# Scores of the first attention layer as three products in half-height tiles, with splits over all partitions and a new order of the program

## The chip, the cores and the metric

The kernel runs on one core of a Trainium2 chip. The metric is device time in microseconds (us) of one execution. The engines are TensorE (PE for its matrix products, PEld for its loads of the stationary operand), VectorE (DVE), ScalarE (ACT), GpSimd (POOL) and SyncE (SP), whose queue issues nearly all DMAs.

## The reference, cut to what matters

Two layers over 256 tokens of width 1024, 16 heads of 64. The change touches the scores of layer 0 (block attention; with 256 tokens there is one block, so it is plain causal attention):

```python
q = rope(rms_norm(split_heads(q, N_HEADS), q_gain), pos)     # per head 256 x 64
k = rope(rms_norm(split_heads(k, N_HEADS), k_gain), pos)
s_own = jnp.einsum('bhcd,bhkd->bhck', qc, k_own)             # scores, contraction of 64
m_own = jnp.broadcast_to(k_pos[None, :] <= q_pos[:, None], (B, H, C, MOBA_BLOCK))
pr = masked_softmax(s * scale, m)
o = merge_heads(pr @ v) * jax.nn.silu(z)
x = x + o @ w_out
gate = jax.nn.sigmoid(rms_norm(x, ple_gate_gain[i]) @ ple_w_gate[i])
x = x + gate * (p[i] @ ple_w_proj[i])
```

Layer 1 is the NSA mixer (compressed, selected and window branches) with the same output and gate parts. Gains of the norms are about 8, so scores are large and are computed to nearly full float32 accuracy.

## The kernel before, in words

Products run in the type fp32r. To keep accuracy every float32 operand is split in two: hi, the value rounded to fp32r (one ScalarE copy), and lo, the rest (one VectorE subtraction); a product is then hi x hi + lo x hi + hi x lo. Weights arrive in pieces of 128 x 1024 (`raw`), are split into `hi` and `lo` tiles of five buffers each, and are multiplied with the split activations `a`, into four PSUM banks named `mm`. PSUM banks `s` (two) take scores, banks `tr` (two) transposes and the products with the values.

Nothing is issued in the order in which it is written. The kernel records all its operations in a `Plan`. `PROGRAM` (line 26) names some 500 steps; where a step stands there sets the priority of its operations. `schedule` (line 263) goes through the operations with costs for each (`cost`, line 187) and places on every engine the one that can start first. A switch of PE between tile shapes is charged there (line 347), and `together` (line 243) keeps a list of operations next to each other on PE. So an edit of a cost or of `PROGRAM` can move any instruction of the kernel; line 399 issues them all, which is why every row of the profile has that line.

Layer 0's attention goes by eight `Pair`s of heads (line 982), each in three steps, and four value steps `V0` to `V3`:

- `A` transposes q and k of two heads into one `tr` bank: head 0 on partitions 0 to 63, head 1 on 64 to 127, columns q (256) then k (256). `stack_moba` (line 968) then builds, for each head j, a tile `qk[:, j]` with the head's hi on its own half of the partitions and its lo on the other half, and a tile `k2` with the halves of k exchanged. That takes two ScalarE copies of 64 x 512, two VectorE subtractions of 64 x 512 and four copies of 64 x 256, which the planner gives to ScalarE or VectorE.
- `S` (line 997) computes, for each head j and each half t of the tokens, two products over all 128 partitions: `qk` x `qk` (hi hi + lo lo) and `qk` x `k2` (the two mixed terms). For t = 0 they have 128 columns, for t = 1 256. That is eight products a pair, `together` by twos. The softmax's maximum and exponential follow on VectorE and ScalarE (`block_exp`, tile `sm`).
- `T` (line 1019) transposes the exponentials into `pt`.
- `V` (`pairs_pv`, line 852) multiplies with the values in tiles of 64 columns, two heads alternating between halves of the array's columns. Plain float32 products such as these show as two records each.

The scores of layer 1 (line 1174) use stacked tiles in the same way as `stack_moba` and are not edited.

Of the kernel before, what the change touches and what calls it, by code (L numbers as in the profile page):

```python
# [7 lines left out]
F32 = mybir.dt.float32  # L8
# [5 lines left out]
P = 128  # L14
T = 256
# [4 lines left out]
SWITCH, POW = 150.0, 2300.0  # L20
NRAW, NHI, NLO, NPT, NA = 5, 5, 5, 9, 9
WARM = 16
WIDE, NARROW = "o0 o1 g0 g1 no0 no1 ng0 ng1", "ng1b"
MARGIN = 100.0

PROGRAM = ("x0 w:c0 c0 x1 w:c1 c1 x2 w:c2 x3 w:c3 x4 w:c4 w:k.0 x5 c2 w:c5 c3 x7 consts tq a.1 x6 a.3 a.5 a.6 w:c6 a.7 w:c7 "
# [24 lines left out]

STORES = 5

# [55 lines left out]
class Plan:  # L109
# [77 lines left out]
    def cost(self, op, views, first):  # L187
        n = first.elems() if isinstance(first, View) else 0
        e, m = op.engine, op.method
        if m == "dma_start":  # L190
            v = first if isinstance(first, View) else op.args[1]
            return v.elems() * 4 * v.ap.ap[0][1]
        if e == "tensor":
            k, c = op.args[1].ap.ap[0][1], op.args[1].ap.ap[1][1]
            op.mode = tuple(128 if x > 64 else 64 if x > 32 else 32 for x in (k, c))
            if m == "transpose":
                return 109.2
            if op.args[1].ap.dtype == mybir.dt.bfloat16:
                return n / 2.4
            if op.args[1].ap.dtype == F32R:  # L200
                return (n + 32) / 2.4 if n > 128 else 110

            return 2 * max(54.6 if op.mode == (128, 64) else 109.2, 2 * n / 2.4 / (2 if op.mode == (128, 64) else 1))
        if e == "gpsimd":
            if op.kwargs.get("op") == OP.pow:
                return (POW if n < 16 else 1300.0) + 130.0 * n
            return 100 + 2.3 * n
        psum = any(self.tags[v.tile.tag]["psum"] for v in views)
        rows = first.ap.ap[0][1]
        half = 110 if rows in (60, 64) and (any(v.box()[0] != first.box()[0] for v in views)  # L210
                                            or psum and first.ap.dtype == F32R and m == "activation") else 0
        if e == "scalar":
            if first.tile.tag == "early":
                return 1500.0
            c = (60 if psum else 110) + 0.833 * max(n, op.args[1].elems())
            return half + c + 93 * sum(isinstance(op.kwargs.get(k), View) for k in ("scale", "bias", "accum_out"))
        if m == "tensor_tensor_reduce":
            return 130 + 1.04 * n
        if m == "reciprocal":
            return 65 + 6.9 * n  # L220
        if m == "tensor_reduce":
            return 65 + 1.04 * op.args[1].elems()
        two = len([v for v in views if v.elems() > 2 and v is not first]) > 1
        if not psum and not two and m in ("tensor_copy", "tensor_scalar"):
            return 70 + half + 0.52 * n + 60 * any(isinstance(x, View) and x.elems() == 1 for x in op.args[2:])
        if m == "tensor_tensor" and args_step(op.args[1]) >= 16:
            return 65 + 1.75 * n
        return 65 + half + 1.055 * n + (65 if m == "scalar_tensor_tensor" and isinstance(op.args[2], View) else 0)
# [192 lines left out]
def trunk(ctx: ExitStack, tc: tile.TileContext, a, out):  # L421
# [543 lines left out]
    def masks_():  # L965
        nc.hold_on(lambda: load_consts(384, CST_N), at["w:" + BEHIND.split()[1]])

    def stack_moba(ps):

        qk = work.tile([P, 1024], F32R, tag="hl", name="qk").rearrange("p (j c) -> p j c", j=2)  # L970
        k2 = work.tile([P, 512], F32R, tag="qk", name="k2").rearrange("p (j c) -> p j c", j=2)
        own = [slice(0, HD), slice(HD, P)]
        for j in range(2):
            o = own[j]
            nc.scalar.activation(qk[o, j], ps[o], AF.Copy)
            nc.vector.tensor_tensor(qk[own[1 - j], j], ps[o], qk[o, j].bitcast(F32), op=OP.subtract)
        for j in range(2):
            nc.copy(k2[own[1 - j], j], qk[own[j], j, T:])
            nc.copy(k2[own[j], j], qk[own[1 - j], j, T:])
        return qk, k2  # L980

    class Pair:


# [4 lines left out]
        def A(self):  # L989
            ps = bank("tr", 2)  # L990
            for i, s in enumerate((self.half.Q, self.half.K)):
                for t in range(2):
                    nc.tensor.transpose(ps[:, (2 * i + t) * P:(2 * i + t + 1) * P],
                                        s[:, t, 2 * self.p:2 * self.p + 2].rearrange("p a d -> p (a d)"), ident)
            self.qk, self.k2 = stack_moba(ps)

        def S(self):
            qk, k2 = self.qk, self.k2
            self.l = work.tile([P, 2, 2], F32, tag="l", name="l")
            ss, self.sm = [bank("s", 2) for _ in range(2)], []  # L1000
            for j in range(2):
                for t in range(2):
                    since = len(nc.ops)
                    for x in range(2):
                        n = t * P + P
                        nc.tensor.matmul(ss[j][:, cuts[t]], qk[:, j, t * P:n], k2[:, j, 0:n] if x else qk[:, j, T:T + n],
                                         start=x == 0, stop=x == 1)
                    nc.together(since)
            for j in range(2):
                sm = work.tile([P, 384], F32, tag="sm", name="sm", bufs=5)  # L1010
                self.sm.append(sm)
# [515 lines left out]
```

## Time and profile before

| | us |
|---|---|
| median of three runs (359.20, 359.52, 360.35) | 359.52 |
| profiled execution, its own time | 360.45 |
| profiled execution, its span | 358.7 |

The span runs from the first to the last instruction of the profiled execution. PE, PEld, DVE and ACT below are busy times; matrix products are pipelined, so a record's duration (some 0.28 us for 256 columns) is longer than the distance to the next start (0.12 us), and it is the distance between starts that tells what a product costs. In groups, `out<-in` names tiles, `128*64` the rows and columns of the array that a product uses, `128x256` the shape of its result; the last two columns are busy us with the mean ns of one, and the idle time before it. `s<-hl` and `s<-qk,hl` are the score products, `tr<-pt,v` the value products, `mm` the projections. In layer 0, `hl` is the buffer of `qk`, and `qk` that of `k2`.

### The profile page before, as it was taken

How to read it: one execution, taken by the hardware profiler on the slowest of the kernel's cores; microseconds unless marked ns; L12 is line 12 of the kernel's file. 1: busy time of each engine (PE TensorE's matmuls, PEld its weight loads, DVE VectorE, ACT ScalarE, POOL GpSimd, SP SyncE). 2: the span in 40 equal slices, each digit the busy share in tenths (PEclk: the TensorE clock that was granted, in tenths of full speed). 3: DMA queues.
4: the chain of work that ended last, by engine and by line, in shares of the span. 5: the costliest groups of instructions: out<-in, count | busy, mean ns of one | idle time of the engine just before them, and what ended most of it. 6: DMA issues, size and time to landing. Idle time of an engine off the chain costs nothing.

```text
span 358.7 us, 6738 instructions
## 1 busy us (share of the span) xinstructions
PE 351.5 (98%) x2329; PEld 308.9 (86%) x2329; DVE 333.9 (93%) x845; ACT 276.2 (77%) x614; POOL 29.1 (8%) x26
## 2 busy tenths in 40 slices
PE   6999999999999999999999999999999999999995
PEld 5888888888999888888889999866998989888885
DVE  3999989999999988989999999999999999999985
ACT  3976599998999864758853988978989999956632
POOL 1033300321000000000004300003000000000100
PEclk9999999999999999999999999999999999999999
DMA  7999665053653456664443725347674332167012
GB/s 219 320 366 275 217 211 192 32 158 133 212 178 116 132 172 172 184 215 147 166 131 95 258 66 174 119 137 273 238 222 156 118 106 74 58 191 221 0 47 73
DMA packets 20770, 58.95 MB, mean 164 GB/s; under 512 B 2560, under 2 KB 6016, under 8 KB 20736
## 3 DMA queue, kind: packets, MB, share of 16 engines
q1 hardware_dynamic: 20160, 58.04, 50.0%
q10 hardware_dynamic: 576, 0.48, 0.4%
q8 instruction: 18, 0.29, 0.3%
q14 instruction: 16, 0.13, 0.1%
HBM read 57.46 MB, written 1.05 MB: 163 GB/s over the span
## 4 chain that ended last, share of the span: by engine, by line
PE 96%; DMA 2%; DVE 0%; ACTq 0%; issue 0%; ACT 0%; DVEq 0%
PE mm L399 77%; PE tr L399 13%; PE s L399 6%; DMA tmp<-in_moba_in 2%; ACTq L399 0%; DVE tmp L399 0%; DVE hi L399 0%; ACT tmp L399 0%; DVEq L1522 0%; DVE xT L399 0%
## 5 line engine op out<-in xcount | busy, mean ns | idle before, releaser
L399 PE MATMUL mm<-a,hi 128*128 128x256 f32 (+1 forms) x656 | 163.4, 327 | 0.0
L399 ACT ACTIVATE hi<-raw 128x1024 fp32r<-128x1024 f32 (+2 forms) x100 | 99.7, 1008 | 35.2 <-PE mm L399 29.5
L399 PE MATMUL mm<-a,lo 128*128 128x256 f32 x448 | 125.5, 284 | 0.0
L399 DVE TENSOR_TENSOR lo<-raw,hi 128x1024 fp32r<-128x1024 f32 (+2 forms) x100 | 115.0, 1159 | 5.9 <-ACT hi L399 5.3
L399 PEld LDWEIGHTS mm<-a,hi 128*128 128x128 f32 x656 | 109.9, 190 | 10.6
L399 PE MATMUL mm<-hi,a 128*128 128x512 f32 (+2 forms) x356 | 101.7, 375 | 1.7 <-DVE hi L399 1.7
L399 PEld LDWEIGHTS mm<-a,lo 128*128 128x128 f32 x448 | 84.4, 190 | 0.6 <-DVE big L399 0.2
L399 PEld LDWEIGHTS mm<-hi,a 128*128 128x128 f32 x356 | 64.2, 190 | 12.8 <-ACT a L399 1.9
L399 PE MATMUL mm<-lo,a 128*128 128x512 f32 (+2 forms) x178 | 63.8, 374 | 0.0
L399 ACT ACTIVATE sm<-sm,nb 128x128 f32<-128x128 f32 (+1 forms) x96 | 42.6, 448 | 3.8 <-DVE nb L399 3.6
L399 PEld LDWEIGHTS mm<-lo,a 128*128 128x128 f32 x178 | 33.0, 188 | 5.4 <-DVE lo L399 0.2
L399 DVE CUSTOM_DVE_ANT_0 sm<-s,cst,nr_q 128x128 f32<-128x128 f32 (+1 forms) x96 | 35.7, 408 | 0.5 <-PE s L399 0.2
L399 ACT ACTIVATE pt<-tr 128x384 f32<-128x384 f32 x48 | 21.7, 484 | 0.6 <-PE tr L399 0.4
L399 ACT ACTIVATE tmp<-tmp 128x256 f32<-128x256 f32 (+3 forms) x26 | 12.1, 471 | 12.9 <-DVE tmp L399 12.7
L399 PE MATMUL tr<-cst,sm 128*128 128x128 f32 x144 | 22.0, 275 | 0.0
L399 POOL TENSOR_TENSOR r_q<-r,neg_half 128x16 f32<-128x16 f32 x5 | 14.6, 2922 | 77.3 <-DVE r L399 77.3
L399 PEld LDWEIGHTS tr<-cst,sm 128*128 128x128 f32 x144 | 16.9, 141 | 3.1 <-ACT sm L399 0.8
L399 ACT ACTIVATE a<-xT,gain_in 128x256 fp32r<-128x256 f32 x31 | 14.5, 498 | 5.2 <-DMA xT<-in_x 3.2
L399 DVE TENSOR_TENSOR hl<-tr,hl 64x512 fp32r<-64x512 f32 x24 | 16.5, 688 | 2.1 <-ACT hl L399 1.5
L399 ACT ACTIVATION_READ_ACCUMULATOR sm<-sm,nb 128x1 f32 x96 | 18.3, 191 | 0.0
L399 DVE TENSOR_SCALAR sm<-sm,l 128x128 f32<-128x128 f32 (+1 forms) x67 | 17.7, 314 | 0.1
L399 POOL TENSOR_TENSOR rstd<-ms,neg_half 128x2 f32<-128x2 f32 x4 | 3.9, 973 | 167.9 <-DVE ms L399 167.9
(167 smaller groups left out, 452.4 us busy)
## 6 DMA issues: line engine op xcount, KB each, us to landing
raw<-in_moba_in SPq DMA_DIRECT2D x28, 512.0 KB, 4.3
raw<-in_nsa_in SPq DMA_DIRECT2D x24, 512.0 KB, 4.5
raw<-in_w_o SPq DMA_DIRECT2D x8, 512.0 KB, 3.7
raw<-in_w_g SPq DMA_DIRECT2D x8, 512.0 KB, 3.9
raw<-in_w SPq DMA_DIRECT2D x8, 512.0 KB, 3.6
raw<-in_w_no SPq DMA_DIRECT2D x8, 512.0 KB, 4.0
raw<-in_w_ng SPq DMA_DIRECT2D x8, 512.0 KB, 4.2
raw<-in_ple_proj SPq DMA_DIRECT2D x4, 512.0 KB, 3.9
```

The source lines that it names most:

```text
L399: getattr(getattr(self.nc, o.engine), o.method)(*[real(x) for x in o.args], **{k: real(x) for k, x in o.kwargs.items()})
```

## The change

`stack_moba` goes. `A` now makes one tile `hl` of 128 x 1024: hi of the whole transposed bank (q and k of both heads, all partitions), then lo. `S` computes three products a head and token half, hi hi, lo hi and hi lo, each over the 64 partitions of its head, with the two heads in turn, and all twelve are kept together. The product lo lo is no longer computed.

```diff
-    def stack_moba(ps):
-        qk = work.tile([P, 1024], F32R, tag="hl", name="qk").rearrange("p (j c) -> p j c", j=2)
-        k2 = work.tile([P, 512], F32R, tag="qk", name="k2").rearrange("p (j c) -> p j c", j=2)
-        own = [slice(0, HD), slice(HD, P)]
-        for j in range(2):
-            o = own[j]
-            nc.scalar.activation(qk[o, j], ps[o], AF.Copy)
-            nc.vector.tensor_tensor(qk[own[1 - j], j], ps[o], qk[o, j].bitcast(F32), op=OP.subtract)
-        for j in range(2):
-            nc.copy(k2[own[1 - j], j], qk[own[j], j, T:])
-            nc.copy(k2[own[j], j], qk[own[1 - j], j, T:])
-        return qk, k2
...
-            self.qk, self.k2 = stack_moba(ps)
+            self.hl = work.tile([P, 1024], F32R, tag="hl", name="hl").rearrange("p (x c) -> p x c", x=2)
+            nc.scalar.activation(self.hl[:, 0], ps, AF.Copy)
+            nc.vector.tensor_tensor(self.hl[:, 1], ps, self.hl[:, 0].bitcast(F32), op=OP.subtract)
...
-            for j in range(2):
-                for t in range(2):
-                    since = len(nc.ops)
-                    for x in range(2):
-                        n = t * P + P
-                        nc.tensor.matmul(ss[j][:, cuts[t]], qk[:, j, t * P:n], k2[:, j, 0:n] if x else qk[:, j, T:T + n],
-                                         start=x == 0, stop=x == 1)
-                    nc.together(since)
+            since = len(nc.ops)
+            for t in range(2):
+                n = t * P + P
+                for q, k in ((0, 0), (1, 0), (0, 1)):
+                    for j in range(2):
+                        r = slice(j * HD, j * HD + HD)
+                        nc.tensor.matmul(ss[j][:, cuts[t]], self.hl[r, q, t * P:n], self.hl[r, k, T:T + n],
+                                         start=q == k, stop=k == 1)
+            nc.together(since)
```

The planner's cost of an fp32r product is halved when the tile has 64 rows and 128 columns, and `PROGRAM` is another list from the step `masks` on; before it, both lists are the same. One line of each, from the start of layer 0's attention:

```diff
-           "w:1q.0 w:1q.3 1q.0 masks w:1k.0 A2 S2 w:1k.2 w:1q.1 w:1q.2 A3 1k.0 1k.1 w:1v.0 S3 1q.1 1q.2 1q.3 1qe A0 1q T2 "
+           "w:1q.0 w:1q.3 1q.0 masks w:1k.0 v A2 S2 A3 w:1k.2 1k.0 1k.1 S3 w:1q.1 w:1q.2 1q.1 1q.2 1q.3 1qe w:1k.3 w:1v.0 "
```

On PE, the first score block (step `S2`) of before stands inside the projections with the weights `hi_116`; `s_156` and `s_157` are the two banks of scores:

```order
L399 MATMUL mm_78<-lo_121,a_107 128x512
L399 MATMUL mm_79<-hi_116,a_107 128x512
L399 MATMUL s_156<-hl_150 128x128
L399 MATMUL s_156<-qk_152,hl_150 128x128
L399 MATMUL s_156<-hl_150 128x256
L399 MATMUL s_156<-qk_152,hl_150 128x256
L399 MATMUL s_157<-hl_150 128x128
L399 MATMUL s_157<-qk_152,hl_150 128x128
L399 MATMUL s_157<-hl_150 128x256
L399 MATMUL s_157<-qk_152,hl_150 128x256
L399 MATMUL mm_79<-hi_116,a_107 128x512
```

The same block of the changed kernel, from its last products of 128 columns on (`s_154` and `s_155` are the two banks):

```order
L399 MATMUL s_154<-hl_150 128x128
L399 MATMUL s_155<-hl_150 128x128
L399 MATMUL s_154<-hl_150 128x256
L399 MATMUL s_155<-hl_150 128x256
...
L399 MATMUL mm_78<-hi_116,a_107 128x512 x2
L399 MATMUL mm_78<-lo_121,a_107 128x512
```

The block now alternates between the two banks, is twelve products long (six of each width), and stands ahead of the first product with `hi_116`. In the whole changed order each of the eight score blocks is one run of twelve, with full-width products before and behind it; the products in tiles of 64 or 60 columns form eight runs before and eight after.

On ACT, the splits for the first two pairs (steps `A2` and `A3`) before; `hl` and `qk` are the tiles of `stack_moba`, `hi` is a split of weights, `sm` the exponentials:

```order
L399 ACTIVATE hl_150<-tr_76 64x512 x2
L399 ACTIVATE qk_152<-hl_150 64x256 x2
L399 ACTIVATE hl_151<-tr_75 64x512
L399 ACTIVATE qk_152<-hl_150 64x256 x2
L399 ACTIVATE hi_114<-raw_124 128x1024
L399 ACTIVATE qk_153<-hl_151 64x256
L399 ACTIVATE hl_151<-tr_75 64x512
```

and in the changed kernel:

```order
L399 ACTIVATE hl_150<-tr_76 128x512
L399 ACTIVATE hl_151<-tr_75 128x512
L399 ACTIVATE hi_114<-raw_124 128x1024
L399 ACTIVATE sm_69,l_152<-sm_69,nb_156 128x128
L399 ACTIVATE sm_69,l_152<-sm_69,nb_156 128x256
```

Two instructions stand where twelve stood (three of the copies lie further down in the order of before), and the split of the next weights and the exponentials of the first pair move up.

More of the change, by code (lines that the diff above doesn't have):

```diff
@@ L22 @@
 WARM = 16
-WIDE, NARROW = "o0 o1 g0 g1 no0 no1 ng0 ng1", "ng1b"
+WIDE, NARROW = " o0 o1 g0 g1 no0 no1 ng0 ng1", "ng1b"
 MARGIN = 100.0
@@ L200, in cost @@
             if op.args[1].ap.dtype == F32R:
-                return (n + 32) / 2.4 if n > 128 else 110
+                return ((n + 32) / 2.4 if n > 128 else 110) / (2 if op.mode == (64, 128) else 1)
             return 2 * max(54.6 if op.mode == (128, 64) else 109.2, 2 * n / 2.4 / (2 if op.mode == (128, 64) else 1))
@@ L994, in A @@
                                         s[:, t, 2 * self.p:2 * self.p + 2].rearrange("p a d -> p (a d)"), ident)
-            self.qk, self.k2 = stack_moba(ps)
+            self.hl = work.tile([P, 1024], F32R, tag="hl", name="hl").rearrange("p (x c) -> p x c", x=2)
+            nc.scalar.activation(self.hl[:, 0], ps, AF.Copy)
+            nc.vector.tensor_tensor(self.hl[:, 1], ps, self.hl[:, 0].bitcast(F32), op=OP.subtract)
         def S(self):
-            qk, k2 = self.qk, self.k2
             self.l = work.tile([P, 2, 2], F32, tag="l", name="l")
             ss, self.sm = [bank("s", 2) for _ in range(2)], []
-            for j in range(2):
-                for t in range(2):
-                    since = len(nc.ops)
-                    for x in range(2):
-                        n = t * P + P
-                        nc.tensor.matmul(ss[j][:, cuts[t]], qk[:, j, t * P:n], k2[:, j, 0:n] if x else qk[:, j, T:T + n],
-                                         start=x == 0, stop=x == 1)
-                    nc.together(since)
+            since = len(nc.ops)
[7 more added lines that the diff above has]
+            nc.together(since)
             for j in range(2):
```

44 rows, old and new, of the table PROGRAM are left out of this document.

## The prediction

> **What bounds the kernel now.** I read the page first, then the busy time by stage, then the waits of the loading side of TensorE, and last the rows around one score block and one value block. The page:
>
> ```profile
> span 358.7 us, 6738 instructions
> PE 351.5 (98%) x2329; PEld 308.9 (86%) x2329; DVE 333.9 (93%) x845; ACT 276.2 (77%) x614; POOL 29.1 (8%) x26
> ```
>
> TensorE (PE) is busy 98% of the span. Where the other 2% lies is read from the busy time by stage; the columns are the stretch, its length, then busy time and instructions of PE, PEld, DVE, ACT, POOL, the granted clock and DMA:
>
> ```profile
> 0.00:44.80 44.80, 42.02 (x194) 34.15 (x195) 38.59 (x75) 28.44 (x42) 10.04 (x14) 1.00 0.83 279
> 44.80:125.88 81.08, 81.08 (x580) 73.17 (x578) 78.61 (x197) 75.48 (x173) 6.01 (x2) 1.00 0.47 152
> 125.88:212.00 86.12, 86.12 (x512) 76.50 (x510) 80.25 (x161) 59.10 (x101) 7.37 (x4) 1.00 0.53 166
> 212.00:314.20 102.20, 102.05 (x801) 89.36 (x800) 100.01 (x335) 90.92 (x258) 4.07 (x5) 1.00 0.45 148
> 354.50:358.70 4.20, 0.00 (x0) 0.00 (x0) 1.38 (x6) 0.51 (x2) 0.00 (x0) 0.79 0.23 72
> ```
>
> The first layer's scores stand in the second stretch, 44.8 to 125.9 us, and there PE is busy for all of it, at full clock. The idle 2.8 us of the first stretch and the last 4.2 us lie before and behind everything that the change moves. A busy PE could still be slowed by late operands, since its records overlap; that would show on the side that loads weights. Its waits in the second stretch, with total, count and longest, are
>
> ```profile
> PEld tr L399 <- ACT pt L399: 0.3, 1, 0.3
> PEld tr L399 <- ACT big L399: 0.2, 1, 0.2
> PEld tr L399 <- issue: 0.2, 1, 0.2
> ```
>
> That is 0.7 us of 81. So the time here is the sum of what PE is given to do. ScalarE (75.5 of 81.1 us) and VectorE (78.6) are nearly full but late for almost nothing.
>
> **The score block as it is.** One pair of heads, with two projection products well before it (start, duration, engine, operation, shape):
>
> ```profile
> 88.83 0.28 PE L399 MATMUL mm<-a,hi 128*128 128x256 f32 x1
> 88.95 0.28 PE L399 MATMUL mm<-a,lo 128*128 128x256 f32 x1
> ...
> 91.22 0.22 PE L399 MATMUL s<-hl 128*128 128x128 f32 x1
> 91.28 0.28 PE L399 MATMUL s<-qk,hl 128*128 128x128 f32 x1
> 91.40 0.33 PE L399 MATMUL s<-hl 128*128 128x256 f32 x1
> 91.57 0.28 PE L399 MATMUL s<-qk,hl 128*128 128x256 f32 x1
> 91.69 0.22 PE L399 MATMUL s<-hl 128*128 128x128 f32 x1
> ...
> 92.15 0.40 PE L399 MATMUL mm<-a,hi 128*128 128x256 f32 x2
> ```
>
> From the first score product at 91.22 to the next projection product at 92.15 are 0.93 us for eight products (the block at 95.02 takes 0.92; I use 0.92), so 0.115 us each, though half of them stream only 128 columns. What a column costs follows from records of two lengths:
>
> ```profile
> L399 PE MATMUL mm<-a,hi 128*128 128x512 f32 x240 | 85.1, 398 | 0.0
> L399 PE MATMUL mm<-a,hi 128*128 128x256 f32 x416 | 78.6, 286 | 0.0
> L399 PE MATMUL tr<-pt,v 128*64 128x256 f32 x96 | 14.8, 386 | 0.0
> L399 PE MATMUL tr<-pt,v 128*64 128x128 f32 x96 | 9.3, 273 | 0.0
> ```
>
> In the split type 256 more columns take 398 - 286 = 112 ns, 0.44 ns a column. The four products of one head stream 768 columns, 0.34 us, and take 0.46. They are held not by streaming but by the load of 128 stationary columns, one each 0.115 us.
>
> **The same block after the change.** Twelve products, six of 128 and six of 256 columns, in pairs: rows 0 to 63 for one head and rows 64 to 127 for the other. No product of before uses half the rows, so its price needs bounds. The nearest rows are the value products, which use half the columns of the array, alternating between two heads in the same way. First, do such pairs overlap? In the rows above 128 more columns take 386 - 273 = 113 ns there, 0.88 ns a column. One value block has 16 records of 256 and 16 of 128 columns, 6144 columns, 5.4 us one after another. It takes half of that:
>
> ```profile
> 122.81 0.39 PE L399 MATMUL mm<-a,hi 128*128 128x512 f32 x1
> 123.13 2.58 PEld L399 LDWEIGHTS tr<-pt,v 128*64 128x64 f32 x32 [0.25 <-ACT big L399]
> 123.13 2.82 PE L399 MATMUL tr<-pt,v 128*64 128x256 f32 x32
> 125.88 0.19 PEld L399 LDWEIGHTS mm<-a,lo 128*128 128x128 f32 x1 [0.17 <-DVE big L399]
> 125.88 0.39 PE L399 MATMUL mm<-a,lo 128*128 128x256 f32 x1
> ...
> 126.11 0.39 PE L399 MATMUL mm<-a,hi 128*128 128x512 f32 x1
> ```
>
> From 123.13 to 125.88 are 2.75 us, so the two halves do work side by side, and I take the same for halves of rows: a pair costs what one product costs. With loads also side by side the body of a block is one load that nothing hides (0.115), three steps of 128 columns that each wait for the next load (0.115 each) and three of 256 columns (0.12 each, the spacing of the rows at 88.83): 0.82 us, against 0.92.
>
> The same rows price going into another shape and out. The product at 122.81 streams 512 columns, 0.23 us, so PE could go on at 123.04 and goes on at 123.13: 0.09 us. On the way out the first product of full width starts at 125.88 and the next only 0.23 us later, not 0.12: its weights could not be loaded ahead, 0.11 us. Between them, the block's 2.75 us are 0.05 to 0.19 more than its columns need (6144 columns at half of 0.88 or at 0.42 to 0.44 ns give 2.56 to 2.70), of which I take 0.10 for the way out. So one visit costs 0.09 + 0.10 + 0.11 = 0.30 us beside its body; the unhidden first load is in the body already. The block then costs 0.82 + 0.30 = 1.12 us against 0.92; **+0.20 us a pair, and +1.6 us for eight**. In the changed order all eight blocks stand alone among full-width products, so each pays both ways; the value and compression blocks in halves of columns are eight visits before and eight after.
>
> The length of a load with 64 rows is not in the trace. Between 0.06 us (half of 0.115) and 0.115, the low end would make the body 0.06 + 3 x 0.06 + 3 x 0.12 = 0.60 and the block 0.90, no change at all; I keep 0.115, since the rows above hold 128 columns fixed and so does the change. The Trainium skill, "TensorE: Matmul & The Clock Gate", section "LDWEIGHTS (loading the stationary operand)", says that a load's time follows its columns, and that one of 32 rows takes as long as one of 128; by it the block is the 1.12 us above, without it 0.90, and no row of this case has fewer than 124 rows to test it.
>
> **The splits.** The diff drops two half-height reads, two half-height subtractions and four copies of a pair, and puts one read and one subtraction over all partitions in their place:
>
> ```profile
> L399 DVE TENSOR_TENSOR hl<-tr,hl 64x512 fp32r<-64x512 f32 x24 | 16.5, 688 | 2.1 <-ACT hl L399 1.5
> L399 ACT ACTIVATE hl<-tr 64x512 fp32r<-64x512 f32 x24 | 14.2, 590 | 0.9 <-PE tr L399 0.5
> L399 ACT ACTIVATE qk<-hl 64x256 fp32r<-64x256 f32 x29 | 11.5, 411 | 0.5
> L399 DVE CAST qk<-hl 64x256 fp32r<-64x256 f32 x3 | 0.9, 288 | 0.1
> L399 DVE TENSOR_TENSOR tmp<-mm,bc 128x512 f32<-128x512 f32 x10 | 6.8, 680 | 0.1
> L399 ACT ACTIVATE tmp<-mm 128x512 f32<-128x512 f32 x10 | 5.6, 586 | 2.2 <-PE mm L399 2.2
> ```
>
> Height costs nothing (688 against 680 ns, 590 against 586). ScalarE loses 16 x 0.59 + 11.5 and gains 8 x 0.59: -16.2 us. VectorE loses 16 x 0.69 + 0.9 and gains 8 x 0.68: -6.5 us. Both are cover that PE's 81.08 of 81.08 us hides; in this stage they can return at most the 0.7 us of waits above, 0.5 of which stand at the value block shown and come back with its change of shape. I count 0.
>
> **The new order.** Every step behind the first score block may move. The numbers of projections, transposes and value products stay, so a different order changes the sum of PE only through waits. In the fourth stretch one real wait is plain:
>
> ```profile
> 255.52 0.28 PE L399 MATMUL mm<-a,hi 128*128 128x256 f32 x1
> 255.94 0.48 PE L399 MATMUL s<-v_1r,hl 128*128 128x256 f32 x2
> ```
>
> 0.42 us between starts, where 0.12 is usual: 0.30 lost. It may go, and others like it may come. From a gain of 1.0 us (this one, the 0.7 of the second stretch) to a loss of as much, I take the gain of this one wait, 0.3 us, since the rows show it to be there and show no second of its size. Weights that the new order asks for earlier wait in buffers; the DMA's share of 0.45 to 0.53 in these stretches leaves room, and the start, where it is 0.83, keeps its order.
>
> Sum: +1.6 + 0 - 0.3 = +1.3. The profiled execution took 360.45 us, 1.75 more than its span, and would take 361.75. The median of the three runs shown is 359.52, 0.9 below it; on that scale the forecast is **360.8 us**, with 360.1 to 362.1 for the order's 1.0 us either way. A difference of less than 0.3% (1.1 us, 358.4 to 360.6) can't be told from none here.
>
> **Rivals.** (a) *Two halves for the price of one, and no toll.* The toll of 0.30 us is read from halves of columns. If going to halves of rows costs nothing, the first load is hidden too, and the body is 3 x 0.115 + 3 x 0.12 = 0.70 us: -0.22 a pair, -1.8 in all, 357.7 us, faster. For it: nothing shows a toll for rows. Against it: the value block pays on both sides though its tiles use all rows, so the toll looks like one of changing shape. It decides from a toll under 0.1 us. The Trainium skill, "TensorEngine Tiling (Array Packing)", gives a factor of up to 2 for a contraction of 64 under "Theoretical Speedup", which is this rival, and says under "Key Properties" that a change of mode drains TensorE, which is the forecast's toll; the value block's 0.09 us agrees with the second.
>
> (b) *Loads take turns.* If the two halves of a pair stream side by side but load one after another, each block is twelve loads of 0.115 and a last product, 1.50 us, and with the toll 1.80: +0.88 a pair, +7.0 in all, 366.5 us. For it: loads already hold the block of before. Against it: the value block's 32 loads fit in its half time; but those have 64 columns, and were not what held it.
>
> (c) *The relief comes back through the order.* With 16 us less on ScalarE and 6.5 on VectorE the new order removes the waits and hides some of the toll behind them: -1.0 to -2.0 on the forecast, 358.8 to 359.8, no difference. Against it: the 0.7 us of waits in that stage are all there is to win, and the other stages' engines get no relief.
>
> **Chances.** Forecast 0.60 (of which 0.34 end slower and 0.26 within 0.3%, since it lies close to that bound), (a) 0.16 (0.13 faster, 0.03 within, for a toll in between or shorter loads), (b) 0.12 (slower), (c) 0.12 (0.08 within, 0.04 faster). Faster 0.17, within 0.3% 0.37, slower 0.46. The range goes down to 357.4, so that (a) is in it, and up to 363.0, the 362.1 with another 0.9 us of waits; only (b) and a little beside it are left out.
>
> **What would show it.** In the changed profile PE stays fully busy from 44.8 us on; a score block takes about 1.12 us from its first record to the next full-width one plus what it lost before it, with its two heads' records starting within a few ns; the next projection's first step is 0.23 us. A block of 0.7 us without gaps shows (a), one of 1.5 or more with loads 0.115 us apart (b). ACT's total falls by 16 us and DVE's by 6.5 with little effect on the span. I am wrong if PE shows new waits of over 2 us in all, or if the span falls by more than a block's change accounts for.

## The result, and the profile after

| | before | after |
|---|---|---|
| median of six runs, us | 359.57 (359.13 to 360.35) | 361.40 (360.95 to 362.81) |
| profiled execution, its own time / its span, us | 360.45 / 358.7 | 361.95 / 360.2 |

The ratio of after to before is 1.0053, with a 95% interval of 1.0036 to 1.0070: the change costs 1.9 us (1.3 to 2.5). Each ratio further below is to the kernel of before, run beside that experiment; its median went from 359.57 to 359.86 us between the sets of runs, so medians from different sets compare only to some 0.3 us. The page of the changed kernel:

```profile
PE 353.5 (98%) x2361; PEld 308.3 (86%) x2361; DVE 326.3 (91%) x831; ACT 259.5 (72%) x580; POOL 31.9 (9%) x26
```

ACT fell by 16.7 us and DVE by 7.6, and the span grew all the same. PE has 32 products more (eight blocks of twelve instead of eight) and is busy 2.0 us longer. The busy time by stage, columns as before:

```profile
44.80:127.00 82.20, 82.20 (x612) 71.87 (x611) 73.27 (x191) 60.18 (x139) 6.01 (x2) 1.00 0.49 153
212.00:314.20 102.20, 101.20 (x791) 88.49 (x791) 98.63 (x331) 92.39 (x262) 4.06 (x5) 1.00 0.43 141
```

In the stage of the scores PE has no gap, as before, now with ScalarE at 60 of 82 us. In the fourth stretch it waits for 1.0 us, where before it waited for 0.15. In the first stretch it waits less than before (1.45 instead of 2.8 us) though both lists are the same there, so spans compare the two executions badly. Two rows that both have are better ends: the last row of four `hi` products ahead of the first score block, the point from which the lists differ, and the last product of all. In the trace of before, with two products of the fourth stretch that come late:

```profile
45.00 1.17 PE L399 MATMUL mm<-hi,a 128*128 128x512 f32 x4
...
214.12 0.52 PE L399 MATMUL mm<-a,lo 128*128 128x256 f32 x3
214.65 0.50 PE L399 MATMUL s<-k_0r,hl 128*128 128x256 f32 x2
...
270.12 0.28 PE L399 MATMUL mm<-a,lo 128*128 128x256 f32 x1
270.39 1.08 PE L399 MATMUL s<-kcB,qk_0r 128*128 128x32 f32 x8
...
354.18 0.28 PE L399 MATMUL mm<-a,lo 128*128 128x256 f32 x1
```

The same two ends after, and between them the first score block and the four waits of the fourth stretch (in brackets the idle time just before the row, and what ended it):

```profile
44.27 1.17 PE L399 MATMUL mm<-hi,a 128*128 128x512 f32 x4
...
46.42 0.61 PE L399 MATMUL mm<-hi,a 128*128 128x512 f32 x2
46.88 0.39 PE L399 MATMUL mm<-lo,a 128*128 128x512 f32 x1
47.20 0.95 PE L399 MATMUL s<-hl 64*128 64x128 f32 x12
48.08 0.73 PE L399 MATMUL mm<-hi,a 128*128 128x512 f32 x2
48.65 0.39 PE L399 MATMUL mm<-lo,a 128*128 128x512 f32 x1
...
216.02 0.36 PE L399 MATMUL s<-k_0r,hl 128*128 128x256 f32 x1 [0.21 <-DVE nb L399]
...
254.96 0.97 PE L399 MATMUL s<-v_1r,hl 128*128 128x256 f32 x4 [0.22 <-DVE hl L399]
...
257.09 0.47 PE L399 MATMUL s<-v_1r,hl 128*128 128x256 f32 x2 [0.21 <-DVE nb L399]
...
271.89 0.52 PE L399 MATMUL s<-kcB,qk_0r 128*128 128x32 f32 x3 [0.35 <-DVE nb L399]
...
355.68 0.28 PE L399 MATMUL mm<-a,lo 128*128 128x256 f32 x1
```

From row to row are 309.18 us before and 311.41 after: +2.23 us. Two sums make it up.

*The blocks.* The product at 46.88 streams until 47.11 (two of its kind take 46.88 - 46.42 = 0.46, 0.23 each) and the block begins at 47.20: 0.09 us for going into half-height tiles. From there to the first full-width product at 48.08 are 0.88. The next two steps together take 48.65 - 48.08 = 0.57 instead of 0.46: 0.11 for a load that could not be made ahead. Together 1.08, against 0.92 before, +0.16. All eight blocks are alike within 0.01 us from first record to the next full-width one. Behind two of them a transpose follows, and there the load costs 0.06 more, not 0.11. Their surplus adds up to 6 x 0.16 + 2 x 0.11 = **+1.18 us**.

*The waits.* PE's idle time in the fourth stretch grew by 1.0 - 0.15 = 0.85 us. PE lost more than that. A record of 256 columns is 0.28 us long where the next start usually comes after 0.12, so 0.16 us are gone before any idle time shows. Counted from start to start, the four late products above come 0.49, 0.50, 0.49 and 0.63 us behind the product ahead of them (0.28 and the idle time), 1.63 us more than four times 0.12. In before three came late, 0.29 us (214.36, the last start of its row, to 214.65), 0.42 (255.52 to 255.94, in the prediction) and 0.27 (270.12 to 270.39), 0.62 us more than three times 0.12. The difference is **+1.01 us**, all of it ahead of scores of the second layer, and in the changed kernel for `nb` and `hl` of VectorE.

1.18 and 1.01 are 2.19 of the 2.23.

### The profile page after: what moved, and what is told of

It reads as the page before. It is cut to its first block, busy times and chain, and to the rows that moved or that the text cites. A ratio compares the mean times of both kernels' runs of the same rounds, so it can differ in the third digit from the quotient of the medians.

```text
span 360.2 us, 6758 instructions
## 1 busy us (share of the span) xinstructions
PE 353.5 (98%) x2361; PEld 308.3 (86%) x2361; DVE 326.3 (91%) x831; ACT 259.5 (72%) x580; POOL 31.9 (9%) x26
## 4 chain that ended last, share of the span: by engine, by line
PE 83%; DVE 9%; DMA 4%; issue 2%; ACT 1%; ACTq 0%; DVEq 0%
PE mm L399 67%; PE tr L399 11%; PE s L399 5%; DVE lo L399 3%; DMA raw<-in_moba_in 2%; DMA raw<-in_nsa_in 1%; DMA tmp<-in_moba_in 1%; DVE tmp L399 1%; DVE sm L399 1%; DVE hl L399 1%; DVE vcB L399 1%; ACT hi L399 1%; DVE k_1r L399 0%; DVE kd_0r L399 0%; DVE ssq L399 0%
## 5 line engine op out<-in xcount | busy, mean ns | idle before, releaser
L399 ACT ACTIVATE hi<-raw 128x1024 fp32r<-128x1024 f32 (+1 forms) x100 | 99.9, 1007 | 42.9 <-PE mm L399 32.4
L399 DVE TENSOR_TENSOR lo<-raw,hi 128x1024 fp32r<-128x1024 f32 (+1 forms) x100 | 115.3, 1159 | 14.4 <-ACT hi L399 14.1
L399 PE MATMUL mm<-a,lo 128*128 128x256 f32 x448 | 124.1, 283 | 0.0
L399 PE MATMUL mm<-lo,a 128*128 128x512 f32 (+2 forms) x178 | 64.7, 376 | 0.0
L399 POOL TENSOR_TENSOR rstd<-ms,neg_half 128x2 f32<-128x2 f32 x4 | 5.7, 1432 | 166.0 <-DVE ms L399 132.9
L399 PE MATMUL tr<-pt,v 128*64 128x256 f32 (+1 forms) x192 | 16.9, 328 | 0.0
```

The source lines that it names most:

```text
L399: getattr(getattr(self.nc, o.engine), o.method)(*[real(x) for x in o.args], **{k: real(x) for k, x in o.kwargs.items()})
```

## The experiments

The theory was that of the forecast: the eight visits to half-height tiles make the loss, about 1.3 us, and the order and the splits add next to nothing. The rivals were that the new order makes the loss, or that the relief of ScalarE and VectorE carries part of the gain back and hides a larger price of the products.

**The parts alone: scores or order.** The first kernel has the new splits and products in the old `PROGRAM`, the second the old ones in the new `PROGRAM` (with the old planner's cost). One line of the edit of the first, on the changed kernel:

```diff
-           "w:1q.0 w:1q.3 1q.0 masks w:1k.0 v A2 S2 A3 w:1k.2 1k.0 1k.1 S3 w:1q.1 w:1q.2 1q.1 1q.2 1q.3 1qe w:1k.3 w:1v.0 "
+           "w:1q.0 w:1q.3 1q.0 masks w:1k.0 A2 S2 w:1k.2 w:1q.1 w:1q.2 A3 1k.0 1k.1 w:1v.0 S3 1q.1 1q.2 1q.3 1qe A0 1q T2 "
```

> The new splits and score products in the list of steps of before. Theory T (toll): each of eight score blocks pays for going into and out of half-height tiles and costs 1.09 us in place of 0.92, so +1.3 us on before, 360.9, whatever the order. Rival O (order): the blocks cost nothing and all of the loss is the new order's, so 359.6, no difference to before. Rival R (relief): the engines freed of 16 us (ScalarE) and 6.5 us (VectorE) give something back, below 359.

Measured: 360.95 us, ratio 1.0045 (1.0030 to 1.0060). The common rows in its trace, and its fourth stretch:

```profile
43.91 1.17 PE L399 MATMUL mm<-hi,a 128*128 128x512 f32 x4
...
354.30 0.28 PE L399 MATMUL mm<-a,lo 128*128 128x256 f32 x1
```

```profile
212.00:314.20 102.20, 102.05 (x801) 89.26 (x801) 99.93 (x335) 91.06 (x258) 4.07 (x5) 1.00 0.43 148
```

From row to row 310.39, +1.21 on before, with PE idle for 0.15 us in the fourth stretch as before. So the loss is there without the new order, in the size of the blocks alone (1.18), and without the new waits. By the ratio it is 1.6 us (1.1 to 2.2), against 1.9 with the new order: the order's part, 0.3 us (-0.5 to 1.1) between the two ratios, is not clear of noise. The relief of the other engines shows no gain in the old order.

> The splits and score products of before in the new list of steps. T: only the waits that the new order has in the second layer remain, about +0.5 (up to 1.0) us on before, 360.1. O: the whole loss, 361.4. R: worse than the changed kernel, over 362, since the new order counts on the freed engines.

Measured: 367.07 us, ratio 1.0220 (1.0200 to 1.0241). The theory missed this by 7 us. Busy time in the stage of the scores and in a part of it, and PE's two longest groups of waits there:

```profile
44.80:127.00 82.20, 78.63 (x531) 70.45 (x530) 76.17 (x197) 68.37 (x158) 9.43 (x2) 0.98 0.45 144
90.00:110.00 20.00, 17.42 (x121) 16.29 (x120) 17.28 (x42) 15.76 (x34) 1.19 (x1) 0.91 0.26 80
```

```profile
PE tr L399 <- DVE k L399: 1.8, 2, 1.5
PE mm L399 <- ACT big L399: 0.8, 1, 0.8
```

PE is idle for 3.6 us here, waiting for VectorE and ScalarE, and the granted clock is 0.98 over the stage. All of that fall lies between 90 and 110 us, at 0.91, which adds at most 0.09 x 20 = 1.8 us, an estimate; why the clock fell is not shown. The rest of the 7.3 us, some 2 us, was not placed. The old splits and products do not fit the new list.

**Half of the new list.** `PROGRAM` was cut behind the step `nq/0`, ahead of the second layer's scores: the new list up to there and the old one behind it (with the new scores), and the other way round with the old scores and later with the new ones. Steps that both halves held were kept once. The seam of the first:

```diff
-           "nvs.1 nvs.2 w:nvw.1 KE w:nkc.1 nq/0 nvs.3 GT VS KE+ QE0 w:nvw.0 QE0+ w:nvw.3 nkc.0 nkc.1 KT1 KT0 0A nvw.0 0S0 "
+           "w:nkc.1 nq/0 nvs.3 GT VS w:nvw.2 nkc.0 w:nvw.0 KE+ QE0 QE0+ nvw.0 KT1 w:nvw.3 KT0 0A 0S0 0T0 0S3 nvw.1 "
```

> The changed kernel, but from the step behind nq/0 on (second layer from its first scores on) the remaining steps stand in the order of before. T: the four waits of 0.4 to 0.5 us before second-layer scores go back to before's, -1.0 us on the changed kernel, 360.4, still +0.9 or more on before through the score blocks. O with the second layer at fault: 359.6. If the waits stay they are not the list's doing: 361.4.

Measured: 361.27 us, ratio 1.0043 (1.0030 to 1.0056). Its trace (the list is a line longer, so line 400 issues):

```profile
44.51 1.17 PE L400 MATMUL mm<-hi,a 128*128 128x512 f32 x4
...
354.97 0.28 PE L400 MATMUL mm<-a,lo 128*128 128x256 f32 x1
```

```profile
212.00:314.20 102.20, 101.84 (x799) 89.31 (x797) 99.91 (x336) 91.94 (x260) 4.07 (x5) 1.00 0.43 145
```

310.46 us from row to row, +1.28: PE's idle time falls to 0.36 us, and the surplus in the trace falls by 0.95 to about that of the first experiment. In times this does not show: the medians of the two kernels, 361.27 and 361.40, lie 0.13 us apart and their intervals overlap. Nor does it show that the second half of the new list makes the waits. The one-visit control further below has the whole new list, and its fourth stretch has the same idle time:

```profile
212.00:314.20 102.20, 101.84 (x797) 88.83 (x795) 99.50 (x333) 92.42 (x262) 4.07 (x5) 1.00 0.42 143
```

In the nine traces with the new list up to this seam it goes from 0.36 to 1.00 us, against 0.15 in before, and the changed kernel's is the largest. So the new list has more waits here in every trace, but the 1.01 us are those of one trace and not confirmed by timing.

> The counterpart: kernel of before up to the step nq/0, then the remaining steps in the new order, with the scores of before. T: only the second layer's waits are new, +0.5 to +1.0 us on before, 360.1 to 360.6. If those waits came from layer 0's order: no difference, 359.6. O: 361.4.

Measured: 366.55 us, ratio 1.0205 (1.0184 to 1.0227), which no theory had. The fourth stretch and PE's waits in it:

```profile
212.00:314.20 102.20, 97.41 (x745) 84.38 (x744) 98.37 (x336) 87.47 (x249) 4.00 (x5) 1.00 0.44 148
```

```profile
PE tr L400 <- ACT sm L400: 2.3, 1, 2.3
PE tr L400 <- ACT tmp L400: 1.6, 1, 1.6
```

4.8 us of waits, in the second layer, where the scores that were changed are long done. The halves of the two lists do not fit each other, which says nothing on the change; why these two steps come late (buffers that come free in another turn, say) is not shown. The run did give a pair of kernels that differ by the new splits and products in the same surroundings:

> The list with the first half of before and the second half of the new one, which lost 2.05% with the scores of before, now with the new splits and products. If the two halves of the lists don't fit together (buffers in another rotation at the seam), the loss stays and the eight blocks add to it: about 367.9. If that loss too came from the engines' load in the first layer: the 361 of the other mixture.

Measured: 368.21 us, ratio 1.0236 (1.0204 to 1.0268), with the same two waits of 2.3 and 1.6 us.

368.21 - 366.55 = 1.66 us lie between the two medians. But the two ratios, their intervals taken as independent, differ by 0.0031 with 0.0039 either way, 1.1 us (-0.3 to 2.5), and in this trace the granted clock is 0.50 from 312.0 to 315.4 us, where the other has 1.00. So this pair agrees with the 1.18 us that the rows of the blocks give and does not show it by itself; the first experiment does, with 1.21 by its rows and 1.1 to 2.2 by its times.

**Do the two heads run side by side?** The loops over heads and products were exchanged, so that one head's six products stand ahead of the other's:

```diff
-            for t in range(2):
-                n = t * P + P
-                for q, k in ((0, 0), (1, 0), (0, 1)):
-                    for j in range(2):
+            for j in range(2):
+                for t in range(2):
+                    n = t * P + P
+                    for q, k in ((0, 0), (1, 0), (0, 1)):
```

> The changed kernel with the same twelve half-height products a pair, but six for one head, then six for the other, instead of the two heads in turn. If pairs in different halves of the rows run side by side (theory T), this loses it: three steps of 0.11 and three of 0.12 for each head, a body of about 1.4 us in place of 0.8, +0.6 us a block and +4.5 to +5 us on the changed kernel, 366. If the queue finds the pairing by itself, or the pairs never overlapped, no difference: 361.4.

Measured: 363.45 us, ratio 1.0105 (1.0081 to 1.0129), 2.05 on the changed kernel and under half of what was expected. The block in its trace:

```profile
47.50 1.23 PE L399 MATMUL s<-hl 64*128 64x128 f32 x12
48.66 0.73 PE L399 MATMUL mm<-hi,a 128*128 128x512 f32 x2
```

1.16 us instead of 0.88; 0.28 x 8 = 2.2, near the 2.05 measured. So the pairs do overlap when they alternate (the block would have no reason to grow otherwise), but why does it grow by so little? The group of score products under way in the 20 ns around 47.775:

```profile
L399 PE MATMUL s<-hl 64*128 64x128 f32 x4 | 0.6, 298 | 0.0
```

Four products of 128 columns are under way, and a head has only three; none of 256 columns has begun. The fourth is the first one of the other head, which is written behind three wider products of the first head and starts ahead of them; `together` had them issued as written. It is so in all eight blocks. PE takes up the free half of the array by itself, ahead of the written order, and so regains part of what the order of the loops gives away.

**The price of a visit.** One extra full-width product of 128 columns (its result is read by nothing) in the middle of each block makes two visits of one; the control has the same line, without the condition, ahead of the loop over `t`. The edit of the first:

```diff
             for t in range(2):
                 n = t * P + P
+                if t:
+                    nc.tensor.matmul(ss[0][:, 384:512], self.hl[:, 0, 0:P], self.hl[:, 0, 0:P], start=True, stop=True)
```

> The changed kernel with one additional full-width product of 128 columns, into unused columns of a score bank, in the middle of each score block: sixteen visits to half-height tiles in place of eight, and eight more products. T: eight times 0.30 for the toll and 0.11 for the product (and a first load that nothing hides, about 0.05), +3.3 to +3.7 us on the changed kernel, 364.9. If switching costs nothing: +0.9, 362.3.

> The control: the same eight additional products, but ahead of each block, where the array is in full width anyway: still eight visits. T: +0.5 to +0.9 us on the changed kernel, 362.1; the difference to the kernel with sixteen visits is the toll, about 2.4 to 2.8 us. If the toll doesn't exist, both kernels take the same.

Measured: 364.36 us, ratio 1.0127 (1.0108 to 1.0145), with sixteen visits; 361.39 us, ratio 1.0050 (1.0032 to 1.0069), with eight. The block of the first:

```profile
46.30 0.39 PE L399 MATMUL mm<-lo,a 128*128 128x512 f32 x1
46.61 1.36 PE L399 MATMUL s<-hl 64*128 64x128 f32 x13
47.91 0.73 PE L399 MATMUL mm<-hi,a 128*128 128x512 f32 x2
```

and of the control, whose group of 13 begins with the extra product:

```profile
46.37 0.39 PE L399 MATMUL mm<-lo,a 128*128 128x512 f32 x1
46.60 1.10 PE L399 MATMUL s<-hl 128*128 128x128 f32 x13
47.63 0.73 PE L399 MATMUL mm<-hi,a 128*128 128x512 f32 x2
```

From the `lo` product to the first `hi` product are 1.61 and 1.26 us: 0.35 for a second visit. In times it is 364.36 - 361.39 = 2.97 us for eight, 0.37 each (the two ratios, their intervals taken as independent, differ by 0.0077 with 0.0026 either way, which is 0.23 to 0.46 us a visit). The times hold more than the visits: PE's idle time in the fourth stretch is 0.75 us in the trace of the first and 0.36 in that of the control. The rows hold a little more too. Without the extra product they give 48.08 - 46.88 = 1.20 us, so it costs 0.06 ahead of a block and 0.41 in its middle, the second visit included. In the middle the product itself takes between those 0.06 and the 0.115 of a load-bound product, which leaves 0.30 to 0.35 us for the visit. The forecast's 0.30, with an unhidden first load beside it that was counted in the body, is of this size.

**Is the relief free?** The forecast counted the shorter splits as nothing. If so, the longer ones could be put back into the changed kernel at no cost: both halves of the split apart, and the four copies, which nothing reads here.

```diff
-            nc.scalar.activation(self.hl[:, 0], ps, AF.Copy)
-            nc.vector.tensor_tensor(self.hl[:, 1], ps, self.hl[:, 0].bitcast(F32), op=OP.subtract)
+            own = [slice(0, HD), slice(HD, P)]
+            for o in own:
+                nc.scalar.activation(self.hl[o, 0], ps[o], AF.Copy)
+                nc.vector.tensor_tensor(self.hl[o, 1], ps[o], self.hl[o, 0].bitcast(F32), op=OP.subtract)
+            k2 = work.tile([P, 512], F32R, tag="qk", name="k2").rearrange("p (j c) -> p j c", j=2)
+            for j in range(2):
+                nc.copy(k2[own[1 - j], j], self.hl[own[j], 0, T:])
+                nc.copy(k2[own[j], j], self.hl[own[1 - j], 1, T:])
```

> The changed kernel with the products as they are, but the splits in half-height pieces again and four copies of 64x256 a pair into a tile that nothing reads: ScalarE and VectorE get back the 16 and 6.5 us. T: both are cover, within 0.5 us of the changed kernel, 361.4. R: if the relief was worth something, the loss is larger than the +0.53% measured, 363 or more.

Measured: 368.07 us, ratio 1.0233 (1.0207 to 1.0259): 6.7 us on the changed kernel, not none. The stage of the scores and PE's waits in it:

```profile
44.80:127.00 82.20, 77.64 (x556) 66.71 (x555) 77.56 (x201) 69.69 (x158) 9.43 (x2) 1.00 0.44 147
```

```profile
PE s L399 <- DVE nb L399: 2.1, 1, 2.1
PE mm L399 <- ACT v L399: 1.5, 1, 1.5
PE tr L399 <- DVE k L399: 0.8, 2, 0.5
```

PE waits for 4.6 us. Over the whole span VectorE is busy for 335.6 us and ScalarE for 273.6, about the 333.9 and 276.2 of before, which had no gap in this stage. The load as a sum does not make the waits, then. Three more kernels take this apart: the same edit in the old `PROGRAM`, only its copies, only its half-height splits.

> The new score products in the order of before, with the copies and half-height splits put back, as in the run that put them back in the new order and lost 6.7 us on the changed kernel. Theory N (the new order needs the freed engines, the old one doesn't): no more than 0.5 us over the new products in the old order without them, 361. Rival M (the additional work costs by itself, wherever it stands): +5 us or more, 366.

> The changed kernel with only the four copies of 64x256 a pair put back (nothing reads them): about 11.5 us, nearly all on ScalarE. If ScalarE is what the new order counts on, most of the 6.7 us lost with copies and half-height splits together, 366 or more. If it is VectorE, or the longer way from transposes to scores, little: 362.

> The changed kernel with only the splits in half-height pieces (two reads of 0.59 us and two subtractions of 0.69 us a pair in place of one each): 4.7 us more on ScalarE, 5.5 us more on VectorE, and the scores of a pair wait 0.6 to 0.7 us longer for their operands. If VectorE or that way is what the new order counts on, most of the 6.7 us, 366; if ScalarE, 362 to 363.

Measured: 364.72 us in the old order, ratio 1.0138 (1.0123 to 1.0154), which is 3.8 on the first experiment and between the two expectations; 362.04 with the copies alone, 1.0059 (1.0043 to 1.0076); 364.05 with the half-height splits alone, 1.0122 (1.0101 to 1.0143). The stage of the scores in the old order, and its longest wait:

```profile
44.80:127.00 82.20, 79.06 (x575) 68.55 (x576) 77.72 (x199) 72.61 (x167) 9.43 (x2) 1.00 0.43 143
```

```profile
PE tr L399 <- DVE k L399: 2.1, 1, 2.1
```

with the copies alone:

```profile
44.80:127.00 82.20, 81.96 (x605) 71.12 (x605) 74.27 (x196) 68.74 (x159) 9.43 (x2) 1.00 0.48 157
```

and with the half-height splits alone:

```profile
44.80:127.00 82.20, 80.77 (x596) 70.02 (x596) 76.19 (x193) 63.93 (x143) 9.43 (x2) 1.00 0.46 151
```

The copies bring ScalarE from 60.2 to 68.7 us here and cost 0.6 us on the changed kernel, within the intervals: ScalarE has room. The half-height splits add 2.9 us to VectorE and 3.8 to ScalarE, lengthen the way from a transpose to its scores by a second read and subtraction, and cost 2.65 us. Both together cost more than their sum (6.7 against 3.3). Whether VectorE's load or the longer way decides isn't told apart by these kernels. The longest waits are for `k` and `nb`, steps of VectorE; `v` and `big` of ScalarE come next. In the old order the same work costs less (3.8 against 6.7), but it is not free there either.

## Why the prediction was right, point by point

- **The sum of PE bounds the stage.** Right: 82.20 of 82.20 us busy in the changed kernel.
- **The block, +0.20 a pair.** Right in mechanism; measured +0.16, and +0.11 where a transpose follows. The way in is 0.09 and the next load 0.11, as priced from the value block. From the first record to the full-width product are 0.88 us, where the body and the way out were given 0.82 + 0.10 = 0.92; by the rows eight blocks cost 1.18 instead of 1.6.
- **A load of 64 rows as long as one of 128.** Right. Groups of loads in the changed kernel, mean ns behind the busy time:

```profile
L399 PEld LDWEIGHTS mm<-a,lo 128*128 128x128 f32 x448 | 84.1, 190 | 0.6
...
L399 PEld LDWEIGHTS s<-hl 64*128 64x128 f32 x96 | 6.0, 186 | 2.1 <-issue 1.3 <-ACT hl L399 0.4 <-ACT v L399 0.2
```

  186 against 190 ns. The rule of the Trainium skill ("TensorE: Matmul & The Clock Gate", "LDWEIGHTS (loading the stationary operand)"), that a load of fewer rows takes the same time and the columns set it, agrees as far as rows go; both groups have 128 columns. Half the rows cost the same load, and that is why the body can't be halved.
- **The splits, counted 0.** The number was right, the reason too wide. ACT fell by 16.7 (forecast 16.2) and DVE by 7.6 (6.5), and in the old order that brought nothing. But "cover" was taken as slack in both directions. Put back, the work costs 2.7 us (half-height splits) to 6.7 (all), and 3.8 us in the old list. A reason may be that the run of twelve products needs both heads' operands early (argued from its order, not tried). One reading was wrong beside this and changes no term: of the 0.7 us of waits on the loading side, only the 0.25 at 123.13 stand at the value block; the 0.3 for `pt` stand at 63.70, ahead of a transpose.
- **The new order, counted -0.3. This step failed, in sign.** The wait that was to go stayed: the two products `s<-v_1r,hl` that start at 255.94 in before, 0.42 us behind the product ahead, start at 257.09 after, 0.49 us behind it, and other waits were added. "A gain of this one wait, 0.3 us" became a loss of 1.01 us in the trace of the changed kernel, at the edge of the 1.0 us that was allowed either way. The forecast looked at what the order could remove and took the size of new waits from nothing. How much of the loss is the order's own stays open: the idle time differs between kernels with the same list, and the times put the order at 0.3 us (-0.5 to 1.1).
- **Sum.** +1.6 + 0 - 0.3 = +1.3 was forecast. The traces give 1.18 + 1.01 = +2.2, the times +1.9 (1.3 to 2.5). By the traces the forecast gave the blocks 0.4 too much and the order 1.3 too little. That these errors have opposite signs, and the sum comes within 0.6 us of the times, is luck. That the change loses is not: the blocks alone do it, in the old order too.
- **Rivals.** (a), no toll: fallen, by the 0.09 and 0.11 of each block and by the 0.37 of a second visit. (b), loads in turn: fallen; a block of twelve loads in turn would be 1.5 us and is 0.88. (c), the relief comes back as a gain through the order: fallen as a gain, but its first half holds. The new order needs the relief (367.07 us with the old splits and products, 368.07 with the work put back) and gains nothing by it on the old one (361.40 against 360.95).

## What to carry to other kernels

Before two half-height products replace one full-height product, ask what holds the full one. Here it was the load of 128 columns, which half the rows do not shorten, so a pair's body fell only by about 0.14 us (1.08 less the 0.30 of the ways in and out and the next load is 0.78, against 0.92), while each visit to another tile shape cost those 0.30: by these two numbers, an estimate that takes the way out as forecast, more than two pairs would have to share a visit, and two banks for scores allow one (not tried). And idle time of an engine off the bound is not slack in both directions: give relief a value of zero, but don't give the same work, put back elsewhere, a price of zero.

## What the runs showed of the hardware that was not expected

- PE began a product on the free half of the rows ahead of three that are written before it. The Trainium skill, "TensorE: Matmul & The Clock Gate", "The mechanism", says that loads may be pulled ahead but that products keep the program's order in their starts; the four products of 128 columns under way at 47.775 us of the exchanged loops disagree with it. The loss of 2.05 us, where 4.5 to 5 were expected of heads one after the other, fits them.
- A full-width product of 128 columns placed right ahead of a block is nearly free: 1.26 us from the `lo` product to the `hi` product with it and 48.08 - 46.88 = 1.20 without it, where a product of the block before took 0.115. It seems to take up part of the way in. The two kernels' times are the same (361.39 and 361.40).
